# A mixture-of-experts layer on one core: biases by row groups, the remainder's matmuls in three batches, and TensorE in program order

## The chip, the core and the metric

The kernel runs on one core of a Trainium2 chip (trn2) and uses its TensorE (matmuls, PE in the profile; its weight loads are PEld), VectorE (DVE), ScalarE (ACT), GpSimd (POOL) and SyncE (SP, which starts the weight loads). The metric is the device time in microseconds of one execution, the median of several runs.

## What is computed

One layer over 1024 latent tokens of width 1024: a mixer (gated linear attention and pooling), and then a mixture of experts, and a final RMSNorm. The change is in the mixture of experts, 32 experts of which each token takes four:

```python
def expert_block(args):
    xblk, e = args
    gu = xblk @ w_gu[e] + b_gu[e]                 # 1024 x 2048
    gate, up = jnp.split(gu, 2, axis=-1)
    gate = jnp.minimum(gate, SWIGLU_LIMIT)
    up = jnp.clip(up, -SWIGLU_LIMIT, SWIGLU_LIMIT)
    act = (up + 1.0) * gate * jax.nn.sigmoid(SWIGLU_ALPHA * gate)
    return act @ w_down[e] + b_down[e]            # 1024 x 1024
```

The results are weighted by the softmax of the token's four router logits and added up token by token.

## The kernel before, in words

The mixer takes about the first 530 us. What follows is the loop of experts, written out 33 times in Python: turn `e` does gate/up of expert `e` and down of expert `e-1`.

**Experts by rank.** The experts are sorted by their number of tokens, on the chip. The 16 largest are called heavy here, the others light; the loop takes them in the order `HHHLLH`, then `LH` twelve times, then `LL`. Each has a main block of 128 tokens. A heavy one has a remainder of 32 tokens more as well, the first expert two of them.

**The main block.** Weights come in chunks of 1 MB, eight for gate/up and four for down, into a ring of eight buffers (`load_to`). Each chunk is split into a high and a low part of type fp32r: a copy on ACT (L131), a subtraction on DVE (L132), into one of three buffers `hl` (`split_to`). A chunk then takes 12 matmuls of 128x128 by 128x512, three for each product (`mm3`), into `pG` (four PSUM banks) or `pD` (two).

**The remainder.** Its 32 tokens use the array's columns in four groups of 32: four matmuls stand side by side, each with a quarter of the output's columns, into `pR` (one bank). It multiplies the unsplit chunks (`RAW`), every two chunks in gate/up and with every chunk in down. An fp32 matmul appears as two records.

**The biases.** `ball` holds the three bf16 parts of `b_gu` for all experts on 96 partitions. At the start of each expert four matmuls of 128 rows (`onehot` by `ball`) put the bias into `pG` (`gu_start`, L1480), and four in column groups into `pR`.

**Transposes and routing.** Inputs come by an indirect gather on POOL (`xg`, `xq`); `prep_x` transposes them for the next expert, `prep_a` the last expert's activation. Every block of transposes, and every routing result (`prep_route`, tile `pq`), lands in the single bank of the pool `ptr`: a block of four transposes is copied by ACT (L1393) and then subtracted by DVE (L1394), and only after this may TensorE write the bank again.

**What sets the order.** A scheduler places each engine's instructions by readiness on a simulated clock, and among ready ones by their place in the program. `T.strict` makes each TensorE instruction follow the one traced before it on that engine. It is on in parts of the mixer and in the last turn (`e == NE`), and off in the rest of the loop. Turn `e`, in the program's text: the bias; then for each of eight chunks `k` the matmuls, followed at k = 0, 1, 2 by `prep_a` of expert e-1, at k = 3, 4, 5 by `prep_x` of expert e+1, at k = 6 by the selection and at k = 7 by the routing of expert e+2; then the four down blocks of expert e-1, ahead of whose first stands the activation of expert e (`act`), and `finish_e` with a scatter on POOL. Ahead of the loop stand the gathers, `route_weights` (`px`, `pyw`, and three casts on ACT) and the weights' routing for the first two experts.

Of the kernel before, what the change touches and what calls it, by code (L numbers as in the profile page):

```python
# [9 lines left out]
F32 = mybir.dt.float32  # L10
# [42 lines left out]
def tile_hybrid_layer(ctx: ExitStack, tc: tile.TileContext, x, c, ctx_in, c_ctx, w_ada, b_ada, norm_mix_w,  # L53
# [867 lines left out]
        V.memset(jcol[32 * j:32 * j + 32], float(j))  # L921
    emod = rp.tile([P, 1], F32, name="emod")
    V.scalar_tensor_tensor(emod, jcol, -32.0, pcol, op0=ALU.mult, op1=ALU.add)
    jeq = rp.tile([P, 4], F32, name="jeq")
    V.tensor_scalar(jeq, io[:, 0:4], jcol, None, op0=ALU.is_equal)
    ltm = rp.tile([P, NE], F32, name="ltm")
# [377 lines left out]
    h2d4 = h2d.rearrange("t (j n) -> (t j) n", j=4)  # L1304
    nslot = [0]

    slots = RS + [MS[0], MS[2], MS[3]] + RX

    def wslot():
# [63 lines left out]
    def slot_weights(i, pq):  # L1373
        n = 1 + nrem[i]
        wc = xp.tile([P, 3], F32, name="wc", tag="wc", bufs=4)
        V.tensor_reduce(wc[:, :n], pq[:, :n, 2:5], axis=mybir.AxisListType.X, op=ALU.add)  # L1376
        R["wc", i] = wc
# [54 lines left out]
        if e > 0:  # L1432
            stream += [("dn", e - 1, k) for k in range(0, KT, 2)]
    RAW, HL, EV = {}, {}, {}
    AHEAD_LOAD, AHEAD_SPLIT = 7, 2
    pos_load, pos_split = [0], [0]

    def load_to(n):
# [29 lines left out]
    def onehot(i, n):  # L1468
        return ohp[:, order[i]:order[i] + 1].to_broadcast([P, n])

    def gu_start(e):
        g = pgu.tile([P, 4, 512], F32, name="pG", tag="g")
        rs = []
        if nrem[e]:
            rs.append(prm.tile([P, 512], F32, name="pR", tag="r"))
        if nrem[e] > 1:
            rs.append(pdn.tile([P, 2, 512], F32, name="pR1", tag="d")[:, 0])
        GU[e] = (g, rs)
        for n in range(4):
            T.matmul(g[:, n], onehot(e, P), ball[:, n * 512:n * 512 + 512], start=True, stop=False)  # L1480
        bf = ball[:, 0:2048].rearrange("p (h n) -> p h n", h=2)
        for r in rs:
            for j in range(4):
                T.matmul(r[32 * j:32 * j + 32], onehot(e, CAPR), bf[:, :, 256 * j:256 * j + 256],
                         start=True, stop=False)

    def gu_chunk(e, k):
        g, rs = GU[e]
        xT = R["xT", e]
        hl = HL.pop(("gu", e, k))  # L1490
        for n in range(4):
            mm3(g[:, n], xT[:, 0, k], xT[:, 1, k], hl[:, 0, n * 512:n * 512 + 512],
                hl[:, 1, n * 512:n * 512 + 512], False, k == KT - 1)
        if k % 2 == 0:
            return
        raws = [RAW.pop(("gu", e, q)).rearrange("p (h n) -> p h n", h=2) for q in (k - 1, k)]
        for r, xq in zip(rs, R["xqT", e]):
            for i, raw in enumerate(raws):
                for j in range(4):
                    T.matmul(r[32 * j:32 * j + 32], xq[:, i, 32 * (k // 2):32 * (k // 2) + 32],  # L1500
                             raw[:, :, 256 * j:256 * j + 256], start=False, stop=(k == KT - 1 and i == 1))

    def act_unit(gate, up, w, tag, bufs):
        g = ap.tile([P, w], F32, name="ag", tag="ag" + tag)
        t = ap.tile([P, w], F32, name="at", tag="at" + tag, bufs=bufs)
        V.tensor_scalar(g, gate, 7.0, None, op0=ALU.min)
        S.activation(g, g, AF.Gelu_apprx_sigmoid)
        V.tensor_scalar(t, up, 1.0, -6.0, op0=ALU.add, op1=ALU.max)
        V.scalar_tensor_tensor(t, t, 8.0, g, op0=ALU.min, op1=ALU.mult)
        return t  # L1510

    def act(e):
        g, rs = GU.pop(e)
        R["act", e] = act_unit(g[:, 0:2].rearrange("p a n -> p (a n)"), g[:, 2:4].rearrange("p a n -> p (a n)"),
                               D, "m", 1)
        R["actq", e] = [act_unit(r[:, 0:256], r[:, 256:512], 256, "r", 2) for r in rs]

    def dn_start(e):
        d = (pgu.tile([P, 4, 512], F32, name="pDl", tag="g")[:, 2:4] if e == NE - 1 else
# [7 lines left out]
    def dn_chunk(e, k0):  # L1527
        d, rs = DN[e]
        aT = R["aT", e]
        raw = RAW.pop(("dn", e, k0)).rearrange("p (k n) -> p k n", n=D)  # L1530
        hl = HL.pop(("dn", e, k0)).rearrange("p h (k n) -> p h k n", n=D)
        for u in range(2):
            k = k0 + u
            for n in range(2):
                mm3(d[:, n], aT[:, 0, k], aT[:, 1, k], hl[:, 0, u, n * 512:n * 512 + 512],
                    hl[:, 1, u, n * 512:n * 512 + 512], k == 0, k == KT - 1)
        for g, (r, aq) in enumerate(zip(rs, R["aqT", e])):
            for u in range(2):
                for j in range(4):
                    T.matmul(r[32 * j:32 * j + 32], aq[:, u, 32 * (k0 // 2):32 * (k0 // 2) + 32],  # L1540
                             raw[:, u, 256 * j:256 * j + 256], start=(g == 0 and k0 + u == 0), stop=(k0 + u == KT - 1),
                             skip_group_check=True)

    def finish_e(e):
        d, rs = DN.pop(e)
# [31 lines left out]
    def final_tables():  # L1577

        F["y"] = ap.tile([P, 2, D], F32R, name="yhl", tag="aT")
        F["to"] = xp.tile([P, D], F32R, name="to", tag="xg2", bufs=1)  # L1580
        row = ap.tile([P, D], F32, name="trow", tag="agm")
        G.iota(row.bitcast(I32), pattern=[[1, D]], base=0, channel_multiplier=0)
        ixf = xp.tile([P, 1], F32, name="ixf")
        V.tensor_copy(ixf, R["ix", NE - 1])
        V.tensor_copy(row, row.bitcast(I32))
        V.tensor_scalar(F["to"], row, ixf, None, op0=ALU.is_equal)

        F["fw"] = ap.tile([P, D], F32, name="fw", tag="asm")
        nc.sync.dma_start(F["fw"], final_norm_w[None, :].broadcast_to([P, D]))
        st = F["st"] = xp.tile([P, 2, D], F32R, name="wb", tag="xT")  # L1590
        S.activation(st[0:96, 1], bdg, AF.Copy)
        G.tensor_tensor(st[32:64, 1], bdg[32:64], st[32:64, 1].bitcast(F32), op=ALU.subtract)
        w3 = ap.tile([P, NT, 3, NE], F32, name="w3", tag="y")
        S.activation(w3, lgn[:, :, None, :].to_broadcast([P, NT, 3, NE]), AF.Copy)
        F["w3"] = w3
# [70 lines left out]
    with tc.high_priority():  # L1666
        for i in range(2):
            if i == 0:
                prep_sel(0, (slice(0, P), slice(P, P + CAPR * nrem[0])))
            pq = ptr.tile([P, 3, 8], F32, name="pq", tag="t")  # L1670
            route_main(i, pq, slice(0, 2))
            gather_main(i, pq)
            if i == 0:
                prep_sel(1, (slice(0, CAP0 + CAPR * nrem[1]),))
            pq = pdn.tile([P, 3, 8], F32, name="pqr", tag="d")
            route_rem(i, pq, slice(5, 7))
            gather_rem(i, pq)
            if i == 0:
                load_to(1)

                tc.keep_in_program_order(G.memset(slots[(nslot[0] + 1) % 8][0:1, 0:1], 0.0))
                load_to(2)
        pinned[0] = True
        split_to(1)
        pinned[0] = False
        for p_ in range(3):
            prep_x(0, p_)
    route_weights()
    dump("posm", posm)
    dump("wfull", lg)  # L1690
    for i in range(2):
        pq = ptr.tile([P, 3, 8], F32, name="pq", tag="t")
        route_main(i, pq, slice(2, 5))
        route_rem(i, pq, slice(2, 5))
        slot_weights(i, pq)
    for e in range(nexp + 1):
        if e < nexp:
            gu_start(e)
            for k in range(KT):
                advance()  # L1700
                gu_chunk(e, k)
                if e > 0 and k < 3:
                    prep_a(e - 1, k)
                if e + 1 < NE and 3 <= k < 6:
                    prep_x(e + 1, k - 3)
                if e + 2 < NE and k == 6:
                    prep_sel(e + 2)
                if e + 2 < NE and k == 7:
                    prep_route(e + 2)
        T.strict = e == NE  # L1710
        if e > 0:
            dn_start(e - 1)
            for k0 in range(0, KT, 2):
                advance()
                with tc.high_priority() if e == NE - 1 else ExitStack():
                    if k0 == 0 and e < nexp:
                        act(e)
                    if e == NE - 1 and k0 >= 2:
                        prep_a(e, k0 // 2 - 1)
                dn_chunk(e - 1, k0)  # L1720
                if e == NE:
                    (final_tables, lambda: final_weights(0), lambda: final_weights(1), int)[k0 // 2]()
            finish_e(e - 1)
            if e == NE - 1:
                final_rows()
        elif nexp:
            act(e)
            route_blocks()
# [152 lines left out]
```

## Time and profile before

| | us |
|---|---|
| median of three runs (2027.07 to 2027.38) | 2027.13 |
| the profiled execution | 2027.01 |
| its span, first to last instruction | 2025.2 |
| PE busy | 1927.8 |
| DVE busy | 1553.9 |
| ACT busy | 1142.8 |
| POOL busy | 339.5 |

Mean granted TensorE clock over the span: 0.974 of full speed. A row of a timeline has the start (us from the span's start), the length of a run of like instructions, engine, line, operation, output tile and inputs, shape and count; in square brackets the engine's idle time ahead of it and what ended it. Ends of matmuls are modelled and overlap, so starts are compared. Some matmul records are missing (one of the four bias matmuls of an expert, for one).

### The profile page before, as it was taken

What the parts mean: (1) busy time and instruction counts of PE and PEld (TensorE: products, weight loads), DVE (VectorE), ACT (ScalarE), POOL (GpSimd) and SP (SyncE); (2) the same over time, 40 slices, a digit from 0 to 9 for tenths busy, and PEclk for the clock granted to TensorE, in tenths of its full rate; (3) what the DMA queues carried; (4) which work ended last, traced back from release to release, by engine and by line L of the source; (5) the groups of instructions that cost most, each with busy time, mean ns of one, the idle gap of its engine ahead of it and who ended that gap; (6) DMA issues with size and microseconds to landing.
All of it is one profiled execution on the core that took longest, in us unless ns stands there. A gap on an engine that the chain in (4) does not pass through costs nothing.

```text
span 2025.2 us, 29313 instructions
## 1 busy us (share of the span) xinstructions
PE 1927.8 (95%) x11361; PEld 1383.1 (68%) x11393; DVE 1553.9 (77%) x1599; ACT 1142.8 (56%) x1264; POOL 339.5 (17%) x241
## 2 busy tenths in 40 slices
PE   7999998998699999999999999999999999999985
PEld 4776775776465677767676676767667676776764
DVE  4486478568776788879788887978878797887886
ACT  4464556644453466656565565656556565655663
POOL 2010043013301111101111110111211111111113
PEclk9999999998699999999999999999999999999997
DMA  9274422243556798978879797887979788797874
GB/s 350 70 294 183 151 75 90 77 166 106 221 218 259 269 337 317 361 272 318 333 263 363 270 363 278 318 331 258 367 274 356 282 319 331 254 372 272 349 262 178
DMA packets 125480, 532.85 MB, mean 263 GB/s; under 512 B 13180, under 2 KB 27312, under 8 KB 90424
## 3 DMA queue, kind: packets, MB, share of 16 engines
q1 hardware_dynamic: 109416, 482.35, 61.9%
q0 software_dynamic: 15344, 48.01, 9.0%
q8 instruction: 91, 1.49, 0.3%
q10 hardware_dynamic: 576, 0.56, 0.1%
q14 instruction: 53, 0.43, 0.1%
HBM read 498.21 MB, written 32.67 MB: 262 GB/s over the span
## 4 chain that ended last, share of the span: by engine, by line
PE 87%; DVE 6%; ACT 2%; issue 2%; DMA 2%; POOL 1%; SPq 0%; POOLq 0%; DVEq 0%; ACTq 0%
PE pG L74 37%; PE pD L74 17%; PE pa L74 13%; PE pR L74 11%; PE pps L79 3%; PE pw L74 2%; PE pt L74 2%; DVE hl L132 1%; PE pt L79 1%; ACT hl L131 1%; PE pDl L74 1%; PE pq L74 1%; DMA ring<-in_w_ada_dram 0%; DMA mix<-in_w_ada_dram 0%; DVE ra L719 0%
## 5 line engine op out<-in xcount | busy, mean ns | idle before, releaser
L74 PE MATMUL pG<-hl,xT 128*128 128x512 f32 x3072 | 765.1, 401 | 0.7 <-ACT xT L1393 0.7
L74 PEld LDWEIGHTS pG<-hl,xT 128*128 128x128 f32 x3072 | 565.8, 188 | 166.5 <-issue 28.9
L132 DVE TENSOR_TENSOR hl<-ring,hl 128x2048 fp32r<-128x2048 f32 (+2 forms) x199 | 397.1, 2008 | 157.9 <-ACT hl L131 156.4
L131 ACT ACTIVATE hl<-ring 128x2048 fp32r<-128x2048 f32 (+2 forms) x199 | 331.5, 1668 | 265.6 <-PE pG L74 136.2
L131 ACT ACTIVATE hl<-mix 128x2048 fp32r<-128x2048 f32 (+1 forms) x146 | 277.5, 1902 | 208.0 <-PE pG L74 103.4
L132 DVE TENSOR_TENSOR hl<-mix,hl 128x2048 fp32r<-128x2048 f32 x144 | 329.7, 2291 | 73.0 <-ACT hl L131 71.5
L74 PE MATMUL pD<-hl,aT 128*128 128x512 f32 x1488 | 380.3, 404 | 0.9 <-ACT aT L1393 0.7
L74 PEld LDWEIGHTS pD<-hl,aT 128*128 128x128 f32 x1488 | 277.8, 189 | 85.5 <-ACT xT L1393 10.9
L132 DVE TENSOR_TENSOR hl<-ringx,hl 128x2048 fp32r<-128x2048 f32 x96 | 221.7, 2309 | 43.9 <-ACT hl L131 43.9
L131 ACT ACTIVATE hl<-ringx 128x2048 fp32r<-128x2048 f32 x96 | 184.5, 1922 | 99.8 <-PE pG L74 56.3
L1559 POOL DMA_INDIRECT acc<-y,ix x31 | 78.2, 2521 | 903.1 <-DVE y L1554 873.5
L74 PE MATMUL pa<-hl,hi 128*128 128x512 f32 x544 | 181.0, 420 | 6.0 <-DVE wsg L760 3.7
L74 PEld LDWEIGHTS pa<-hl,hi 128*128 128x128 f32 x544 | 103.1, 198 | 32.0 <-DVE wsg L760 4.8
L74 PE MATMUL pa<-hl,lo 128*128 128x512 f32 x272 | 109.3, 415 | 6.0 <-DVE lo L818 6.0
L74 PE MATMUL pa<-hi,hl 128*128 128x512 f32 (+1 forms) x288 | 95.8, 396 | 1.0 <-ACT hi L400 1.0
L1355 POOL DMA_INDIRECT xg<-h2d,ix x32 | 67.8, 2120 | 143.3 <-DVE wc L1376 130.5
L1393 ACT ACTIVATE aT<-pps 128x512 fp32r<-128x512 f32 x62 | 36.4, 587 | 63.7 <-PE pps L79 63.7
L1564 POOL DMA_INDIRECT acc<-yq,ixr x17 | 43.8, 2579 | 152.3 <-DVE hl L132 75.1
L74 PEld LDWEIGHTS pa<-hi,hl 128*128 128x128 f32 x288 | 55.1, 193 | 16.3 <-issue 2.7
L74 PEld LDWEIGHTS pa<-hl,lo 128*128 128x128 f32 x272 | 53.3, 199 | 18.8 <-DVE lo L818 6.4
L74 PE MATMUL pR<-ring,xqT 128*32 128x512 f32 x408 | 65.8, 599 | 0.0
L1394 DVE TENSOR_TENSOR aT<-pps,aT 128x512 fp32r<-128x512 f32 x62 | 42.5, 685 | 19.7 <-ACT aT L1393 19.7
(386 smaller groups left out, 2119.2 us busy)
## 6 DMA issues: line engine op xcount, KB each, us to landing
ring<-in_w_gu_dram SPq DMA_DIRECT2D x96, 1024.0 KB
mix<-in_w_gu_dram SPq DMA_DIRECT2D x96, 1024.0 KB
ringx<-in_w_gu_dram SPq DMA_DIRECT2D x64, 1024.0 KB
ring<-in_w_down_dram SPq DMA_DIRECT2D x48, 1024.0 KB
mix<-in_w_down_dram SPq DMA_DIRECT2D x48, 1024.0 KB
ringx<-in_w_down_dram SPq DMA_DIRECT2D x32, 1024.0 KB
ring<-in_w_in_dram SPq DMA_DIRECT2D x32, 512.0 KB
ring<-in_w_ada_dram SPq DMA_DIRECT2D x16, 1024.0 KB
```

The costliest lines, as they stand in the source:

```text
L74: i = nc.tensor.matmul(*a, **k)
L79: i = nc.tensor.transpose(*a, **k)
L131: S.activation(hl[:, 0], src, AF.Copy)
L132: i = eng.tensor_tensor(hl[:, 1], src, hl[:, 0].bitcast(F32), op=ALU.subtract)
L1355: nc.gpsimd.indirect_dma_start(out=xg, out_offset=None, in_=h2d, in_offset=bass.IndirectOffsetOnAxis(ap=ix[:, 0:1], axis=0))
L1393: S.activation(dst[:, 0, part], pp, AF.Copy)
L1394: V.tensor_tensor(dst[:, 1, part], pp, dst[:, 0, part].bitcast(F32), op=ALU.subtract)
L1559: nc.gpsimd.indirect_dma_start(out=acc, out_offset=bass.IndirectOffsetOnAxis(ap=ix[:, 0:1], axis=0), in_=y, in_offset=None, compute_op=ALU ...
L1564: nc.gpsimd.indirect_dma_start(out=acc4, out_offset=bass.IndirectOffsetOnAxis(ap=ixr[g][:, 0:1], axis=0), in_=yq, in_offset=None, compute_ ...
```

## The change

- `bias_rows` is new. Once, ahead of the loop, it sorts the biases by rank with matmuls: `bq[32 n + 4 j + i, q]` is part i of columns 512 n to 512 n + 511 of the bias of rank 8 q + j. `gu_bias` then adds an expert's bias by four matmuls of 32 rows each, in four row groups and four banks, behind chunk 1 (light) or 3 (heavy).
- The remainder's gate/up matmuls run in two batches, behind chunks 3 and 7, the first together with their bias; those of down in one batch behind the last block.
- So the ring's buffers are free later, and loads run five chunks ahead in place of seven in the program's text.
- The remainder's activation comes ahead of the main one.
- `T.strict` is on from the loop's start to its end.
- Routing of expert e+2 stands behind the second down block of turn e (from e = 1 on).
- `fw` shares the buffer of `bq`.

```diff
+    rsel = rp.tile([P, 2, 8], F32, name="rsel")
+    rhot = rp.tile([P, 8], BF16, name="rhot")
...
+    V.scalar_tensor_tensor(rhot, rsel[:, 0], 4.0, rsel[:, 1], op0=ALU.is_lt, op1=ALU.mult)
...
+    bq = ap.tile([P, 4, 512], BF16, name="bq", tag="bq")
+    def bias_rows():
+        perm = tp.tile([P, NE, 4], BF16, name="perm")
+        V.memset(perm, 0.0)
+        for i in range(3):
+            V.tensor_copy(perm[32 * i:32 * i + 32, :, i], eqr[32 * i:32 * i + 32])
+        flat = perm.rearrange("p r i -> p (r i)")
+        for q in range(4):
+            pb = ptr.tile([P, 512], F32, name="pbq", tag="t")
+            for n in range(4):
+                T.matmul(pb[32 * n:32 * n + 32], flat[0:96, 32 * q:32 * q + 32], ball[0:96, n * 512:n * 512 + 512],
+                         start=True, stop=True)
+            S.activation(bq[:, q], pb, AF.Copy)
...
-    AHEAD_LOAD, AHEAD_SPLIT = 7, 2
+    AHEAD_LOAD, AHEAD_SPLIT = 5, 2
...
-        for n in range(4):
-            T.matmul(g[:, n], onehot(e, P), ball[:, n * 512:n * 512 + 512], start=True, stop=False)
...
+    def gu_bias(e):
+        g, rs = GU[e]
+        q, j = divmod(order[e], 8)
         for n in range(4):
+            rows = slice(32 * n, 32 * n + 32)
+            T.matmul(g[:, n], rhot[rows, j:j + 1].to_broadcast([32, P]), bq[rows, q], start=False, stop=False)
...
-                hl[:, 1, n * 512:n * 512 + 512], False, k == KT - 1)
-        if k % 2 == 0:
+                hl[:, 1, n * 512:n * 512 + 512], k == 0, k == KT - 1)
+        if k == (3 if rs else 1):
+            gu_bias(e)
+        if k % 4 < 3:
             return
...
+            if k == 3:
                 for j in range(4):
+                    T.matmul(r[32 * j:32 * j + 32], onehot(e, CAPR), bf[:, :, 256 * j:256 * j + 256],
+                             start=True, stop=False)
+            for q, raw in raws:
...
     def act(e):
         g, rs = GU.pop(e)
+        R["actq", e] = [act_unit(r[:, 0:256], r[:, 256:512], 256, "r", 2) for r in rs]
         R["act", e] = act_unit(g[:, 0:2].rearrange("p a n -> p (a n)"), g[:, 2:4].rearrange("p a n -> p (a n)"),
                                D, "m", 1)
-        R["actq", e] = [act_unit(r[:, 0:256], r[:, 256:512], 256, "r", 2) for r in rs]
...
+        if k0 < 6:
+            return
+        raws = [RAW.pop(("dn", e, q)).rearrange("p (k n) -> p k n", n=D) for q in (0, 2, 4, 6)]
...
-        F["fw"] = ap.tile([P, D], F32, name="fw", tag="asm")
+        F["fw"] = ap.tile([P, D], F32, name="fw", tag="bq")
...
+    bias_rows()
     route_weights()
...
+    T.strict = True
     for e in range(nexp + 1):
...
-                if e + 2 < NE and k == 7:
+                if e + 2 < NE and k == 7 and e == 0:
                     prep_route(e + 2)
-        T.strict = e == NE
...
                 dn_chunk(e - 1, k0)
+                if k0 == 2 and e + 2 < NE:
+                    prep_route(e + 2)
```

## Rows read from the trace of the kernel before

**Rows 1.** The page's part 1: each engine's busy time, share, instructions.

```profile
PE 1927.8 (95%) x11361; PEld 1383.1 (68%) x11393; DVE 1553.9 (77%) x1599; ACT 1142.8 (56%) x1264; POOL 339.5 (17%) x241
```

**Rows 2.** By stretch, one period: engines' busy us, clock, DMA share, GB/s.

```profile
884.66:973.11 88.45, 88.35 (x512) 62.64 (x513) 72.75 (x52) 53.11 (x38) 12.40 (x7) 1.00 0.84 312
```

**Rows 3.** Timeline of PE, this period: three chunks ahead of transposes.

```profile
932.19 8.63 PE L74 MATMUL pG<-hl,xT 128*128 128x512 f32 x36
940.66 0.60 PE L79 MATMUL pps<-ident,at 128*128 128x128 f32 x4
```

**Rows 4.** The same timeline: the remainder's bias between two blocks of transposes.

```profile
960.96 0.60 PE L79 MATMUL pps<-ident,xg 128*128 128x128 f32 x4
961.32 4.44 PE L74 MATMUL pG<-hl,xT 128*128 128x512 f32 x18
965.69 0.40 PE L74 MATMUL pR<-mix,ohp 128*32 128x512 bf16 x4
966.02 2.84 PE L74 MATMUL pG<-hl,xT 128*128 128x512 f32 x11
968.69 0.38 PE L79 MATMUL ppr<-ident,xq 128*128 128x128 f32 x2
```

**Rows 5.** The same timeline: a bias, a down block, the next transposes.

```profile
913.07 1.04 PE L74 MATMUL pG<-mix,ohp 128*128 128x512 bf16 x3
913.75 3.15 PE L74 MATMUL pD<-hl,aT 128*128 128x512 f32 x12
916.74 0.60 PE L79 MATMUL pps<-ident,xg 128*128 128x128 f32 x4
```

**Rows 6.** The same timeline: first and last gate/up remainder, last down remainder.

```profile
884.95 1.92 PE L74 MATMUL pR<-ring,xqT 128*32 128x512 f32 x16
...
906.13 1.06 PE L74 MATMUL pR<-ring,xqT 128*32 128x512 f32 x6
...
959.40 1.07 PE L74 MATMUL pR<-ring,aqT 128*32 128x256 f32 x16
```

**Rows 7.** Timeline of all engines: transposes, their bank held long.

```profile
1020.25 1.92 ACT L131 ACTIVATE hl<-mix 128x2048 fp32r<-128x2048 f32 x1 [0.88 <-PE pG L74]
1020.28 0.60 PE L79 MATMUL pps<-ident,at 128*128 128x128 f32 x4
...
1022.07 0.58 ACT L1393 ACTIVATE aT<-pps 128x512 fp32r<-128x512 f32 x1
1022.19 2.29 DVE L132 TENSOR_TENSOR hl<-mix,hl 128x2048 fp32r<-128x2048 f32 x1 [0.43 <-ACT hl L131]
...
1024.40 0.69 DVE L1394 TENSOR_TENSOR aT<-pps,aT 128x512 fp32r<-128x512 f32 x1
```

**Rows 8.** Timeline of all engines: other transposes, bank held briefly.

```profile
889.79 0.60 PE L79 MATMUL pps<-ident,at 128*128 128x128 f32 x4
...
891.06 0.69 DVE L1394 TENSOR_TENSOR aT<-pps,aT 128x512 fp32r<-128x512 f32 x1 [1.45 <-ACT aT L1393]
```

**Rows 9.** Timeline of PE where the loop of experts begins.

```profile
543.02 1.22 PE L74 MATMUL pG<-hl,xT 128*128 128x512 f32 x2 [0.74 <-ACT xT L1393]
...
548.66 0.44 PE L79 MATMUL ppr<-ident,xq 128*128 128x128 f32 x2 [0.24 <-ACT xqT L1400]
...
558.76 0.61 PE L74 MATMUL pyw<-pbd,wT 128*128 128x128 f32 x4
...
570.51 0.92 PE L74 MATMUL pq<-info,sel 128*128 128x3 bf16 x72
...
576.99 0.65 PE L74 MATMUL pq<-info,sel 128*128 128x3 bf16 x40
```

**Rows 10.** DMA issues: tiles, queue and count, us from issue to landing.

```profile
xg<-h2d,ix POOLq DMA_INDIRECT x32, 10.6
```

**Rows 11.** Waits of SP in the loop: us in total, times, longest.

```profile
SPq L1446 <- PE pR L74: 505.9, 124, 22.5
```

**Rows 12.** Tile pG, a reader: ns min/median/max, first and last start.

```profile
L1506 DVE TENSOR_SCALAR ag<-pG x32: 1202/1217/1224, 585.7 to 1958.2; 128x1024 f32<-128x1024 f32 x32
```

More of the change, by code (lines that the diff above doesn't have):

```diff
@@ L923, in tile_hybrid_layer @@
     V.scalar_tensor_tensor(emod, jcol, -32.0, pcol, op0=ALU.mult, op1=ALU.add)
+    rsel = rp.tile([P, 2, 8], F32, name="rsel")
+    rhot = rp.tile([P, 8], BF16, name="rhot")
+    V.scalar_tensor_tensor(rsel[:, 0], io[:, 0:8], -4.0, emod.to_broadcast([P, 8]), op0=ALU.mult, op1=ALU.add)
+    V.tensor_scalar(rsel[:, 1], rsel[:, 0], 0.0, None, op0=ALU.is_ge)
+    V.scalar_tensor_tensor(rhot, rsel[:, 0], 4.0, rsel[:, 1], op0=ALU.is_lt, op1=ALU.mult)
     jeq = rp.tile([P, 4], F32, name="jeq")
@@ L1478, in gu_start @@
         GU[e] = (g, rs)
+    def gu_bias(e):
+        g, rs = GU[e]
+        q, j = divmod(order[e], 8)
         for n in range(4):
-            T.matmul(g[:, n], onehot(e, P), ball[:, n * 512:n * 512 + 512], start=True, stop=False)
[L1481 to L1485, printed above, removed]
+            rows = slice(32 * n, 32 * n + 32)
+            T.matmul(g[:, n], rhot[rows, j:j + 1].to_broadcast([32, P]), bq[rows, q], start=False, stop=False)
     def gu_chunk(e, k):
@@ L1492, in gu_chunk @@
             mm3(g[:, n], xT[:, 0, k], xT[:, 1, k], hl[:, 0, n * 512:n * 512 + 512],
-                hl[:, 1, n * 512:n * 512 + 512], False, k == KT - 1)
-        if k % 2 == 0:
+                hl[:, 1, n * 512:n * 512 + 512], k == 0, k == KT - 1)
+        if k == (3 if rs else 1):
+            gu_bias(e)
+        if k % 4 < 3:
             return
-        raws = [RAW.pop(("gu", e, q)).rearrange("p (h n) -> p h n", h=2) for q in (k - 1, k)]
+        raws = [(q, RAW.pop(("gu", e, q)).rearrange("p (h n) -> p h n", h=2)) for q in range(k - 3, k + 1)]
+        bf = ball[:, 0:2048].rearrange("p (h n) -> p h n", h=2)
         for r, xq in zip(rs, R["xqT", e]):
-            for i, raw in enumerate(raws):
+            if k == 3:
                 for j in range(4):
-                    T.matmul(r[32 * j:32 * j + 32], xq[:, i, 32 * (k // 2):32 * (k // 2) + 32],
-                             raw[:, :, 256 * j:256 * j + 256], start=False, stop=(k == KT - 1 and i == 1))
+                    T.matmul(r[32 * j:32 * j + 32], onehot(e, CAPR), bf[:, :, 256 * j:256 * j + 256],
+                             start=True, stop=False)
+            for q, raw in raws:
+                for j in range(4):
+                    T.matmul(r[32 * j:32 * j + 32], xq[:, q % 2, 32 * (q // 2):32 * (q // 2) + 32],
+                             raw[:, :, 256 * j:256 * j + 256], start=False, stop=(q == KT - 1))
     def act_unit(gate, up, w, tag, bufs):
@@ L1529, in dn_chunk @@
         aT = R["aT", e]
-        raw = RAW.pop(("dn", e, k0)).rearrange("p (k n) -> p k n", n=D)
         hl = HL.pop(("dn", e, k0)).rearrange("p h (k n) -> p h k n", n=D)
@@ L1536, in dn_chunk @@
                     hl[:, 1, u, n * 512:n * 512 + 512], k == 0, k == KT - 1)
+        if k0 < 6:
+            return
+        raws = [RAW.pop(("dn", e, q)).rearrange("p (k n) -> p k n", n=D) for q in (0, 2, 4, 6)]
         for g, (r, aq) in enumerate(zip(rs, R["aqT", e])):
-            for u in range(2):
+            for k in range(KT):
                 for j in range(4):
-                    T.matmul(r[32 * j:32 * j + 32], aq[:, u, 32 * (k0 // 2):32 * (k0 // 2) + 32],
-                             raw[:, u, 256 * j:256 * j + 256], start=(g == 0 and k0 + u == 0), stop=(k0 + u == KT - 1),
-                             skip_group_check=True)
+                    T.matmul(r[32 * j:32 * j + 32], aq[:, k % 2, 32 * (k // 2):32 * (k // 2) + 32],
+                             raws[k // 2][:, k % 2, 256 * j:256 * j + 256],
+                             start=(g == 0 and k == 0), stop=(k == KT - 1), skip_group_check=True)
     def finish_e(e):
```

## The prediction, made before the changed kernel was run

> **What bounds the kernel now.** I read the page's busy times by engine first, then those of one stretch of the loop of experts, then TensorE's timeline in one period of that loop, and last, in the timeline of all engines, how long a transposed block holds the one PSUM bank it lands in.
>
> TensorE is busy for nearly all of the span [rows 1]. Inside the loop it has no gap: 88.35 of 88.45 us [rows 2]. That is one period, a heavy expert and a light one; there are 16 such pairs. DVE is busy for 72.75 us of the same stretch and the DMA share is 0.84. So the loop is worth what TensorE's own work is worth, as long as nothing makes TensorE stand. The scheduler brought this about: it lets TensorE take whatever is ready, and so puts a transposed block where its bank has long been free. Ahead of the transposes at 940.66 stand three chunks, 36 matmuls [rows 3], since the transposes before them, though the program text has one chunk there. From these rows one matmul takes (940.66 - 932.19)/36 = 0.235 us and a chunk of 12 takes 2.82; a block of four transposes takes 961.32 - 960.96 = 0.36 us [rows 4].
>
> **What the change takes away.** A pair now holds:
> - two biases of four full-width matmuls. From 913.07 to 916.74 are 3.67 us; less 12 x 0.235 that is 0.85 us for one [rows 5], 0.21 a matmul;
> - visits to 32-column mode. From 960.96 to 968.69 are 7.73 us; less 0.36 and 29 x 0.235 the four small bf16 matmuls cost 0.555 us [rows 4]. They run side by side, so they stream for 0.21 and the way in and out costs 0.345. I count nine such visits in the period: five with gate/up remainders, from 884.95 to 906.13 and broken up by transposes, one with routing, two with down remainders, the later at 959.40 [rows 6], and the one with the remainder's bias at 965.69 [rows 4].
>
> After it a heavy expert has two gate/up batches (the first holds the bias) and one down batch, and routing keeps its visit: four in place of nine. 5 x 0.345 = 1.73 us. The remainder matmuls themselves stay as many.
>
> The trace has no bias of four row groups with bf16. I bound it below by 0.21 (all four at once, no way in or out) and above by 4 x 0.21 + 0.345 = 1.19 (no overlap at all). I take 0.555, the same four matmuls side by side in columns [rows 4], which is the nearest row. That saves 0.295 for each expert, 0.59 a pair. Together 2.32 us a pair, **-37 us** over 16.
>
> A page states that price too. The Trainium skill, "TensorE: Matmul & The Clock Gate", Part 3, tells of four row tiles (32 rows, 512 columns) that ran 3.07 times as fast as one after another. By it the bias would cost an estimated 0.85/3.07 = 0.28 us, and the total would lie 9 us lower. No run here shows it.
>
> **What the fixed order adds, in the loop.** All transposes and routing share the one bank of pool ptr. In program order one chunk lies between the blocks for k = 0 and 1 (the activation's two halves) and between those for k = 3 and 4 (the next expert's input). So the second wants the bank 0.36 + 2.82 = 3.18 us after the first began. The trace shows when it is free: the block begins at 1020.28, ACT has begun the next split 0.03 us before (the chunk's end freed its buffer), copies at 1022.07, DVE takes that split's subtraction first and ends the block's at 1024.40 + 0.69 [rows 7]. That is 4.81 us, and TensorE in a fixed order would stand for 1.63. The bound from below is nothing: at 889.79 DVE was through after 1.96 us [rows 8], because no split had begun. I take 4.81, since in the fixed order every block comes right behind a chunk, as there, and each chunk's end starts a split. Places:
> - k = 0 to 1, experts 1 to 31: 15 heavy ones at 1.63; 16 light ones with the bias between, 1.63 - 0.555 = 1.08. Together 42 us.
> - k = 3 to 4: in heavy experts the batch lies between chunk and block, so the split is over: nothing. 15 light ones at 1.63: 25 us.
> - the remainder's transposes behind these (k = 2 and 5), 32 places between nothing and 1.63: while TensorE stood, ACT and DVE worked off the split, so I take a quarter of a us, 8 us.
>
> Together **+75 us**, between 0 and 119.
>
> **And ahead of the loop.** The first pinned matmul stands behind the last one traced before it, the second expert's routing for the weights. Now the first expert's gate/up begins at 543.02 while that routing comes at 570.51 and 576.99 [rows 9]. Its chain must now end first: bias_rows' four rounds through the same bank (a block of four small matmuls 0.4 [rows 4], a copy of 128x512 0.6 [rows 7], two hops: some 1.2 each, half of them in the wait for the first gather), px and pyw, then 11.75 us from pyw to the first routing (three casts, two subtractions, two splits between them on ACT), then 2 us of routing. From the last small transposes at 548.66 that makes 549 + 2.4 + 1.5 + 11.75 + 2 = 567, or 24 us late. Some 3 us of that work stood inside the first expert, and its loads and splits will be ready, which I put at 4. I take **+17**, between 10 (casts alone) and 31 (the chain no faster than it was, 577.6).
>
> **Edits I cost at nothing.** Routing for expert e+2 goes two down blocks later: its matmuls, then DVE's index (behind an operation of the activation and a split's, up to 3 us) and POOL's gather, ahead of this expert's scatter as before. Its first use is two down blocks and four chunks on, 6 x 2.82 = 17 us; a gather took 10.6 us from issue to landing (the median) [rows 10], so 3 us are left; without them each late us costs 31. The remainder's activation first: three short DVE operations ahead of the main one, hidden by the 11 us of down work ahead of the next gate/up. Loads five ahead in place of seven: buffers free in fours behind a batch. SP already waits for remainder matmuls, 124 times for gate/up alone [rows 11], and a batch of four chunks (11.3 us) covers four loads of 1 MB at the 312 GB/s of [rows 2] but for 2 us; four more chunks lie ready then. The final weight's row only loads later, some 50 us ahead of its use. The three small DVE operations for rhot are in the 17.
>
> **Sum.** 2025.2 us of span, 1.8 around it: 2027.0, as the median of the runs, 2027.1. -37 + 75 + 17 = +55: **2082 us**.
>
> **The rivals.**
> A, faster. The stalls hang on one order: DVE takes the split's subtraction ahead of the block's. Where DVE is more than 0.6 us behind when the split comes, the block's, which is earlier in the program, is ready too and goes first; the bank is then free in about 3 us and nothing stands. Against it: in the period DVE idles for 16 us. For it: a faster TensorE leaves it less, and the releases differ by 2.9 us already [rows 7, 8]. It decides below some 0.7 us of stall per place. With none of the 75 us the time is 2027 - 37 + 17 = 2007, or 2000 with the short way into the loop, and 1990 if that way costs nothing.
> B, no change: stalls of about 20 us in all, 2027.
> C, slower still. DVE falls behind in down: three operations of the activation and one like them for y, 1.22 us each [rows 12], and four splits of 2.29 [rows 7] are 14.0 us against 11.3 of matmuls. Two splits made ahead cover the 2.7 us; where that lead is gone, up to 1 us for each expert comes on top, about 2110. Or the row groups do not run side by side, so the change does not do what it says: 32 x (1.19 - 0.555) = 20 us more, 2102.
>
> **How the numbers follow.** The forecast has 0.53, A 0.30, B 0.05, C 0.12. Slower by over 0.2% (4 us, about what a measurement of this kernel can tell) takes the forecast and C. The range reaches down through most of A to 1992 and up to 2106, short of C's worst; the forecast's own range is 2050 to 2105.
>
> **What would show it.** Right: TensorE's waits name pps behind the DVE subtraction L1394, 1 to 1.7 us each, some 45 times; a pair takes about 90 us in place of 88.45, with 86 of work; the first gate/up begins near 565; four 32-column visits a pair. Wrong: TensorE still busy for all of a period, of 86 us; or the waits name hl, xg or the loads.

## The result and the profile after

The kernel after takes **2081.45 us** (median of 4 runs, 2080.88 to 2083.54) against 2027.1 before: 1.0269 times as long, 95% interval 1.0256 to 1.0282. The forecast was 2082. The sum came out within 1 us, but its terms did not: the saved work was larger than its term, the added time was larger too, and part of it had no term; the errors cancelled. The times of the experiments below are medians too, that of e11 without one run of 4667.8 us.

Busy time by engine, the page's first part of the kernel after; it answers to [rows 1]:

```profile
span 2079.1 us, 29348 instructions
...
PE 1878.8 (90%) x11409; PEld 1372.6 (66%) x11409; DVE 1552.2 (75%) x1606; ACT 1146.5 (55%) x1268; POOL 361.9 (17%) x241
```

TensorE works 49 us less than before and takes 54 more. So it stands for some 100 us more. What for, the waits of TensorE in the kernel after (what it waited for: us in total, times, longest):

```profile
PE pps L79 <- DVE aT L1416: 51.0, 31, 2.3
PE pps L79 <- DVE xT L1416: 27.0, 16, 1.7
...
PE pps L79 <- DVE at L1539: 6.6, 1, 6.6
PE pw L79 <- ACT w L1626: 6.2, 1, 6.2
...
PE pq L74 <- ACT info L1248: 5.4, 1, 5.4
PE ppr L79 <- DVE xT L1416: 4.8, 3, 1.7
...
PE pblk L74 <- DVE nbb L1269: 4.2, 1, 4.2
```

The first two rows are the wait that was forecast: a block of transposes waits for the one bank until DVE has subtracted the block before. One of the 16 in the second row (1.5 us) stands ahead of the loop; in the loop it is 76.5 us in 46 places. The single waits below are at the loop's entry and end.

Busy time by stretch, before (from the fourth expert's gate/up to the last, and from there to the end) and after (one pair; then the same two stretches); the columns are us, then busy us of PE, PEld, DVE, ACT and POOL, the granted clock, the DMA share and GB/s:

```profile
705.61:1956.80 1251.19, 1249.61 (x7139) 892.99 (x7164) 1033.24 (x720) 757.90 (x526) 196.28 (x85) 1.00 0.84 315
1956.80:2025.20 68.40, 39.06 (x161) 30.22 (x159) 48.78 (x35) 28.71 (x33) 22.50 (x21) 0.79 0.46 170
```

```profile
898.75:988.72 89.97, 84.94 (x517) 61.67 (x513) 72.63 (x52) 53.14 (x37) 15.52 (x6) 1.00 0.81 307
...
723.17:2002.88 1279.71, 1205.45 (x7171) 879.92 (x7168) 1029.34 (x718) 757.80 (x525) 219.08 (x84) 1.00 0.82 309
2002.88:2079.09 76.21, 42.41 (x160) 32.96 (x159) 48.25 (x35) 28.83 (x33) 22.09 (x21) 0.78 0.45 166
```

This is the whole account of 54 us. Up to the fourth expert it is 723.17 - 705.61 = **+17.6**. In the loop TensorE's work falls by 44.2 and its standing rises from 1.6 to 74.3, together **+28.5**. The end is **+7.8** longer. A pair takes 89.97 in place of 88.45 [rows 2], 5.0 of it standing.

One light expert in the loop, the timeline of the kernel after (start, us, engine, operation; in brackets the idle time before it and what ended it):

```profile
947.58 0.60 PE L79 MATMUL pps<-ident,at 128*128 128x128 f32 x4
947.78 1.92 ACT L131 ACTIVATE hl<-ring 128x2048 fp32r<-128x2048 f32 x1 [0.88 <-PE pG L74]
947.79 2.28 DVE L132 TENSOR_TENSOR hl<-ringx,hl 128x2048 fp32r<-128x2048 f32 x1
...
949.60 0.58 ACT L1415 ACTIVATE aT<-pps 128x512 fp32r<-128x512 f32 x1
949.99 2.28 DVE L132 TENSOR_TENSOR hl<-ring,hl 128x2048 fp32r<-128x2048 f32 x1
...
950.91 0.39 PE L74 MATMUL pG<-bq,rhot 32*128 32x512 bf16 x4
...
952.19 0.68 DVE L1416 TENSOR_TENSOR aT<-pps,aT 128x512 fp32r<-128x512 f32 x1
...
952.93 0.66 PE L79 MATMUL pps<-ident,at 128*128 128x128 f32 x4 [1.62 <-DVE aT L1416]
```

The block begins at 947.58. ACT's copy of it is done at 949.60 + 0.58 = 950.18, but DVE took up a split at 949.99 and comes to the block at 952.19. The bank is free at 952.87, 5.29 us after the block began, in place of the 4.81 of [rows 7], and the bias in between (four matmuls side by side, 0.39 us) does not hide the rest.

### The profile page after: what moved, and what is told of

The parts are those of the page before. It is cut to its first block, busy times and chain, and to the rows that moved or that the text cites. A ratio compares the mean times of both kernels' runs of the same rounds, so it can differ in the third digit from the quotient of the medians.

```text
span 2079.1 us, 29348 instructions
## 1 busy us (share of the span) xinstructions
PE 1878.8 (90%) x11409; PEld 1372.6 (66%) x11409; DVE 1552.2 (75%) x1606; ACT 1146.5 (55%) x1268; POOL 361.9 (17%) x241
## 4 chain that ended last, share of the span: by engine, by line
PE 67%; DVE 15%; issue 9%; ACT 7%; DMA 1%; POOL 1%; DVEq 0%; SPq 0%; POOLq 0%; ACTq 0%
PE pG L74 26%; PE pa L74 12%; PE pD L74 11%; PE pR L74 9%; DVE hl L132 6%; ACT hl L131 6%; PE pps L79 2%; PE pw L74 2%; PE pt L74 2%; DVE aT L1416 1%; DVE sel L1348 1%; PE pt L79 1%; DVE xT L1416 1%; DMA mix<-in_w_ada_dram 0%; PE ppr L79 0%
## 5 line engine op out<-in xcount | busy, mean ns | idle before, releaser
L132 DVE TENSOR_TENSOR hl<-ring,hl 128x2048 fp32r<-128x2048 f32 (+2 forms) x199 | 397.9, 2007 | 168.3 <-ACT hl L131 167.1
L74 PE MATMUL pD<-hl,aT 128*128 128x512 f32 x1488 | 365.5, 400 | 0.2 <-DVE hl L132 0.2
L1377 POOL DMA_INDIRECT xg<-h2d,ix x32 | 62.1, 1940 | 895.7 <-DVE ix L1373 439.3
L1591 POOL DMA_INDIRECT acc<-y,ix x31 | 104.5, 3370 | 176.7 <-DVE y L1586 176.7
L79 PE MATMUL pps<-ident,at 128*128 128x128 f32 x256 | 40.6, 282 | 57.6 <-DVE aT L1416 51.0
L79 PEld LDWEIGHTS pps<-ident,at 128*128 128x128 f32 x256 | 29.6, 141 | 73.6 <-DVE aT L1416 62.3
L1415 ACT ACTIVATE xT<-pps 128x512 fp32r<-128x512 f32 x64 | 37.7, 588 | 59.1 <-PE pps L79 56.5
L79 PE MATMUL pps<-ident,xg 128*128 128x128 f32 x256 | 41.1, 284 | 30.7 <-DVE xT L1416 27.0
L79 PEld LDWEIGHTS pps<-ident,xg 128*128 128x128 f32 x256 | 29.9, 143 | 55.3 <-DVE xT L1416 33.9
```

What stands on the lines that cost most here:

```text
L74: i = nc.tensor.matmul(*a, **k)
L79: i = nc.tensor.transpose(*a, **k)
L132: i = eng.tensor_tensor(hl[:, 1], src, hl[:, 0].bitcast(F32), op=ALU.subtract)
L1377: nc.gpsimd.indirect_dma_start(out=xg, out_offset=None, in_=h2d, in_offset=bass.IndirectOffsetOnAxis(ap=ix[:, 0:1], axis=0))
L1415: S.activation(dst[:, 0, part], pp, AF.Copy)
L1591: nc.gpsimd.indirect_dma_start(out=acc, out_offset=bass.IndirectOffsetOnAxis(ap=ix[:, 0:1], axis=0), in_=y, in_offset=None, compute_op=ALU ...
```

## The experiments

Ten kernels were built on one of the two and timed in turn with the kernel before (2027.2 to 2027.8 us in each group).

**e1, the order undone.**

```diff
-    T.strict = True
     for e in range(nexp + 1):
...
+        T.strict = e == NE
```

> The kernel after, with TensorE's order in the loop left to the scheduler again (the last turn as before); row-group biases, the batches in the program text, five loads ahead and the later routing stay. By its instruction list the scheduler cuts the batches up again: 132 groups of remainder matmuls in the loop where the kernel before has 138 and the kernel after 48. My theory (the order costs some 105 us in stalls and at its two ends, and it is also what keeps the batches whole): no waits on pps, first gate/up near 545, of the 37 us of saved work only the bias is left, 32 x 0.3 to 0.46 = 9 to 15 us: 2010 to 2020. Rival 1 (batches pay without the order too): 1985 to 1995. Rival 2 (the cost is in the other edits, shorter load-ahead, later routing or bias rows): 2060 to 2085.

Measured: 2027.24 us, 1.0001 (0.9991 to 1.0010) of before. Neither theory's number. The stalls are gone, so the order makes them, but so is most of what the work saved: a pair takes 88.0, against 88.45 [rows 2].

```profile
875.90:963.90 88.00, 87.89 (x515) 62.33 (x512) 72.97 (x52) 52.87 (x37) 15.46 (x7) 1.00 0.85 313
```

The batches of the program text are only batches if TensorE runs them in the text's order: in the trace, other matmuls part the remainder's into 107 groups in e1 and 120 in the kernel before, but 49 in the kernel after. So the two halves of this change can't be priced apart from each other in a free order.

**e2, the order alone**, on the kernel before.

```diff
+    T.strict = True
     for e in range(nexp + 1):
...
-        T.strict = e == NE
```

> The kernel before with nothing but TensorE in program order from the loop's start; remainder after every second chunk, full-width biases at an expert's start, routing behind the last chunk. My theory (order alone makes the stalls: a block follows a block after one chunk): waits on pps behind DVE of 1 to 1.7 us in 40 to 50 places, a pair of 92 to 94 us, first gate/up 15 to 22 us late: 2100 to 2150. Rival (the stalls come with the changed work, that is with batches that free loads and splits in bursts): waits on pps under 20 us in all, only the entry is dear: 2045 to 2060.

Measured: 2108.32 us, 1.0393 (1.0376 to 1.0411), the theory's time. The stalls need none of the changed work.

```profile
PE pps L79 <- DVE aT L1394: 27.3, 16, 1.7
PE pps L79 <- DVE xT L1394: 27.0, 16, 1.7
PE pD L74 <- DVE hl L132: 10.8, 14, 1.2
```

```profile
905.54:997.40 91.86, 87.55 (x511) 61.27 (x513) 72.67 (x52) 53.27 (x37) 13.28 (x7) 1.00 0.82 300
```

In the loop there are 31 such waits, not 46: here a heavy expert has a batch between its first two blocks. A second reading is new: TensorE works 87.55 us in this pair against 88.35 [rows 2] on the same matmuls. The order as such saves it 0.8 us of work.

**e4, two chunks between blocks.**

```diff
-                if e > 0 and k < 3:
-                    prep_a(e - 1, k)
-                if e + 1 < NE and 3 <= k < 6:
-                    prep_x(e + 1, k - 3)
+                if e > 0 and k in (0, 2):
+                    prep_a(e - 1, k // 2)
+                if e + 1 < NE and k in (4, 6):
+                    prep_x(e + 1, k // 2 - 2)
+                if e < 2 and k == 7:
+                    prep_x(1, 2) if e == 0 else prep_a(0, 2)
...
                 dn_chunk(e - 1, k0)
+                if k0 == 0 and e + 1 < NE:
+                    prep_x(e + 1, 2)
+                if k0 == 4 and 1 < e < NE:
+                    prep_a(e - 1, 2)
```

> The kernel after with the same blocks of transposes two chunks apart in the program text: the activation's halves behind gate/up chunks 0 and 2, the next input's behind 4 and 6, the remainders' transposes in down. Nothing else. My theory (the one bank of the transposes comes free 4.8 to 5.1 us after a block begins; with two chunks the next block wants it after 6.0): the 78 us of waits on pps are gone, a pair takes 85 us, first gate/up as late as in the kernel after: 1998 to 2010. Rival 1 (ACT or DVE can't keep up and the wait moves to the splits hl): a pair of 88 to 90, 2050 to 2080. Rival 2 (half comes back as waits on xg or the loads): 2025 to 2045.

Measured: **1992.64 us**, 0.9824 (0.9807 to 0.9840) of before, 89 us below the kernel after. No wait for the bank is left in the loop, and none came in its place:

```profile
880.57:965.05 84.48, 84.48 (x516) 61.90 (x512) 72.55 (x52) 52.66 (x37) 14.20 (x6) 1.00 0.86 327
...
716.90:1918.00 1201.10, 1198.89 (x7171) 883.00 (x7168) 1028.14 (x718) 751.05 (x525) 203.42 (x84) 1.00 0.87 329
```

TensorE stands for 2.2 us in 1201. My theory holds, with a time 5 us below its range; both rivals fall, though DVE is busy for 86% of the pair. The pair's 84.48 is also the clean price of the work: 3.97 us less than before's 88.45 [rows 2].

**e5, only DVE's order.** A block's subtraction goes ahead of the split's behind it; by the traces, the orders of TensorE, ACT and POOL are those of the kernel after.

```diff
-        V.tensor_tensor(dst[:, 1, part], pp, dst[:, 0, part].bitcast(F32), op=ALU.subtract)
+        i = V.tensor_tensor(dst[:, 1, part], pp, dst[:, 0, part].bitcast(F32), op=ALU.subtract)
+        if pinned[0]:
+            tc.keep_in_program_order(i)
...
     for e in range(nexp + 1):
+        pinned[0] = 0 < e < NE - 1
...
-        split_to(ci + AHEAD_SPLIT)
+        split_to(ci + AHEAD_SPLIT + pinned[0])
```

> The kernel after with one thing moved, DVE's order: a block's subtraction stands ahead of the split's that follows that chunk's end, where the kernel after has it behind. TensorE's and ACT's orders are the same as after. My theory (the block's subtraction is held up by the split's 2.28 us ahead of it in DVE's order, and that makes the stall): the bank is free 3.0 to 3.2 us after a block begins, waits on pps under 15 us in place of 78, 2005 to 2020. Rival 1 (the split, now 0.7 us later, is what TensorE waits for next): waits on hl of 20 to 70 us, 2030 to 2075. Rival 2 (ACT's copy behind ACT's cast is the holder): waits on pps stay above 50 us, 2060 to 2085.

Measured: 2029.02 us, 1.0003 (0.9993 to 1.0013) of before, 52 us below the kernel after. The timeline of the same place, a light expert, and TensorE's longest wait:

```profile
934.29 0.60 PE L79 MATMUL pps<-ident,at 128*128 128x128 f32 x4
...
936.31 0.58 ACT L1415 ACTIVATE aT<-pps 128x512 fp32r<-128x512 f32 x1
936.92 0.69 DVE L1416 TENSOR_TENSOR aT<-pps,aT 128x512 fp32r<-128x512 f32 x1
937.53 2.28 DVE L132 TENSOR_TENSOR hl<-ring,hl 128x2048 fp32r<-128x2048 f32 x1
937.61 0.39 PE L74 MATMUL pG<-bq,rhot 32*128 32x512 bf16 x4
...
937.94 0.66 PE L79 MATMUL pps<-ident,at 128*128 128x128 f32 x4
```

```profile
PE pD L74 <- DVE hl L132: 20.3, 15, 1.6
```

DVE is at the block 0.03 us after ACT's copy, the bank is free 3.3 us after the block began, and the next block starts without a wait. So DVE's order is what makes the stall, as the theory says. But the theory's time is missed by 9 us: the split that was passed over is late in down, 20.3 us in 15 places, which is rival 1 at its lower bound. A pair takes 86.8, 2.3 more than in e4; 1.6 of it is this wait.

**e6 and e7, the fixed order for turns 1 to 30 only**, on e4 and on the kernel after.

```diff
-    T.strict = True
     for e in range(nexp + 1):
+        T.strict = 0 < e < NE - 1
...
+        T.strict = 0 < e < NE - 1 or e == NE
         if e > 0:
             dn_start(e - 1)
```

> The kernel with the blocks two chunks apart (e4), and TensorE's fixed order kept for turns 1 to 30 only: the first expert's gate/up with the route_blocks traced behind it, and turn 31, are left to the scheduler as in the kernel before (the very last turn is fixed in both). My theory (the entry costs 22 to 24 us, route_blocks 5 and more at half clock, the last expert's activation and final weights 8 to 13): first gate/up near 545, last gate/up to end of the span 68 us, 1953 to 1966. Rival (the late entry hides work that must be done anyway, and the loop is then waiting for splits or gathers): first gate/up near 545, but 1975 to 1990.

> The kernel after with TensorE's fixed order kept for turns 1 to 30 only, its blocks one chunk apart as they are. My theory (stalls in the loop and costs of the ends are separate and add): the waits on pps behind DVE stay at 70 to 78 us, 35 to 39 us less at the ends: 2042 to 2050. Rival (the two overlap; the stalls absorb part of the ends' cost): 2055 to 2075.

Measured: e6 **1981.03 us**, 0.9772 (0.9759 to 0.9785) of before, 12 below e4; e7 2064.95, 1.0185 (1.0169 to 1.0201), 16 below the kernel after. Both times are the rivals'; the reason put to e7's, that the stalls in the loop absorb it, is not what happened, since e6 has none. In e6, from the first gate/up to the fourth expert, and the end:

```profile
543.40:710.20 166.80, 153.47 (x1108) 98.39 (x1108) 114.39 (x121) 83.53 (x67) 16.23 (x9) 0.94 0.64 241
...
1910.90:1979.20 68.30, 39.04 (x162) 30.14 (x160) 49.14 (x35) 28.71 (x33) 22.47 (x21) 0.81 0.53 198
```

The end's 7 us come back in full: 68.30, as before. Of the entry little does. The first gate/up begins at 543.40 (543.02 before), but TensorE then stands 13 us inside the stretch, and the fourth expert begins at 710.20, 6.7 earlier than in e4 and 4.6 later than before. The waits moved from ahead of the first expert to behind it:

```profile
594.61 0.92 PE L74 MATMUL pq<-info,sel 128*128 128x3 bf16 x72 [4.26 <-ACT info L1248]
...
599.85 1.12 PE L79 MATMUL pps<-ident,xg 128*128 128x128 f32 x4 [1.41 <-DVE xT L1416]
...
608.38 0.31 PE L74 MATMUL pblk<-linc,nbb 32*32 32x32 f32 x2 [3.27 <-DVE nbb L1269]
```

**e8, full-width biases** and **e9, a batch behind each chunk**, both on e4.

```diff
-            T.matmul(g[:, n], rhot[rows, j:j + 1].to_broadcast([32, P]), bq[rows, q], start=False, stop=False)
+            T.matmul(g[:, n], onehot(e, P), ball[:, n * 512:n * 512 + 512], start=False, stop=False)
```

```diff
-        if k % 4 < 3:
-            return
-        raws = [(q, RAW.pop(("gu", e, q)).rearrange("p (h n) -> p h n", h=2)) for q in range(k - 3, k + 1)]
+        raws = [(q, RAW.pop(("gu", e, q)).rearrange("p (h n) -> p h n", h=2)) for q in (k,)]
...
-            if k == 3:
+            if k == 0:
```

> The kernel with the blocks two chunks apart (e4), and the bias as four full-width matmuls at the same place; bias_rows is still run ahead of the loop. My prediction's term (0.85 against 0.555, 32 times): 9 us more than e4, 2001 to 2003. The rows of the kernel after (the four row groups end 0.75 us behind the chunk's last matmul, of which the way in and out is most): as much or less, 3 to 9 us. By the Trainium skill's factor of three: 18 us, 2010 to 2012.

> The kernel with the blocks two chunks apart (e4), and the gate/up remainder behind each chunk in place of each four: the same matmuls, eight visits to 32-column mode in a heavy expert in place of two. Down stays in one batch. My prediction's term (0.345 us a visit, 96 more): 33 us, 2023 to 2028. Rival 1 (a visit costs nothing, TensorE overlaps it): under 5 us. Rival 2 (each visit also drains what stands behind, 0.5 us and more): 2040 to 2055.

Measured: e8 2005.46 us (ratio 0.9892, 0.9876 to 0.9907), 12.8 over e4, which makes 0.40 us for each of 32 biases. e9 2035.57 us (1.0040, 1.0024 to 1.0055), 42.9 over e4, 0.45 for each of 96 visits. One pair of e8, and one of e9:

```profile
883.00:968.40 85.40, 85.40 (x516) 62.41 (x512) 72.59 (x52) 52.66 (x37) 14.21 (x6) 1.00 0.86 323
```

```profile
891.40:978.50 87.10, 86.65 (x516) 60.97 (x512) 72.37 (x52) 52.76 (x37) 14.21 (x6) 1.00 0.84 318
```

By the pairs it is (85.40 - 84.48)/2 = 0.46 a bias and (87.10 - 84.48)/6 = 0.44 a visit. Both are over the terms of the prediction, 0.295 and 0.345. e8's time lies between that of the prediction's term and that of the factor of three, e9's between its forecast and rival 2. The factor of three of the Trainium skill ("TensorE: Matmul & The Clock Gate", Part 3) would have made the bias's gain an estimated 18 us. It agrees as far as the four row groups do run side by side (0.39 us from the first's start to the last's end, above), but the gain is 13. That the way into their mode and out of it makes the difference is not shown by itself.

**e10 and e11, the entry again.** e10 is e6 with bias_rows moved behind the first two experts' slot weights; e11 is e10 with the fixed order from turn 2.

```diff
-    bias_rows()
     route_weights()
...
         slot_weights(i, pq)
+    bias_rows()
```

```diff
-        T.strict = 0 < e < NE - 1
+        T.strict = 1 < e < NE - 1
```

> The kernel e6 (blocks two chunks apart, fixed order for turns 1 to 30) with bias_rows moved behind route_weights and the first two experts' slot weights in the program. In e6 the rounds of bias_rows took the transposes' one bank ahead of px and pyw, which came at 579 and 585 in place of 554 and 559, and TensorE stood for them at the end of the first expert; the second began at 608.8 against 588.9 before. My theory (that order is the whole delay): px near 555, the routing of the weights near 570, second expert at 592 to 600, 1965 to 1974. Rival (the first expert's free order leaves the next input's blocks for the end whatever stands first): second expert at 604 or later, 1975 to 1985.

> As e10, and TensorE's fixed order begins one turn later, with the third expert, so that the second expert's blocks, its routing and route_blocks can go between matmuls as in the kernel before. My theory (what is left of the entry's cost is the fixed order of turn 1): second expert at 589 to 593, third within 61 us of it as before, 1958 to 1968. Rival (in a free turn 1 the batches are cut up and visits cost what the waits did): within 4 us of e10.

Measured: 1983.00 us (0.9782, 0.9769 to 0.9794) and 1984.08 (0.9789, 0.9776 to 0.9801): no better than e6, and both times the rivals'. In e10 the routing of the weights comes at 572.63, near the 570 expected, and the second expert still begins at 608.0; TensorE now waits ahead of it for DVE's part of a block:

```profile
572.63 0.92 PE L74 MATMUL pq<-info,sel 128*128 128x3 bf16 x72
...
599.01 1.12 PE L79 MATMUL pps<-ident,xg 128*128 128x128 f32 x4 [5.63 <-DVE xT L1416]
```

In e11 the second expert begins at 594.4, but the third at 662.7, where it begins in e6 (662.6) and e10 (662.8) too; before it was 650.8. So my theory fell twice: what I moved was late, but was not what set the third expert. From the second expert's first gate/up to the third's, e11 and then e6:

```profile
594.39:662.75 68.36, 60.67 (x425) 38.91 (x425) 47.58 (x67) 28.55 (x24) 8.42 (x4) 0.93 0.42 147
```

```profile
608.83:662.57 53.74, 53.27 (x377) 36.29 (x375) 39.38 (x44) 27.45 (x21) 5.45 (x2) 0.97 0.48 180
```

e11 is 14.4 us ahead when the second expert begins, and loses it there again: 7.4 us to more work (the remainder's matmuls stand in seven groups, in e6 in three), as its rival has it, and 7.2 to standing, most of it in one wait for DVE's part of a block:

```profile
651.79 0.59 PE L79 MATMUL ppr<-ident,at 128*128 128x128 f32 x2 [5.15 <-DVE xT L1416]
```

What would bring the third expert to 650.8 again was not found; these 12 us stay open.

## Why the prediction was right, and by which steps

**What bounds the kernel: right.** e4 shows it from the other side: with the waits away its span is 85.7 us shorter than that of the kernel after, 79.0 of them TensorE's standing. The five loads ahead and the later routing, costed at nothing, are in e4 too, where no wait for loads or gathers is left from the fourth expert on.

**The saved work: too small.** The prediction put it at 2.32 us a pair; e4 shows 3.97. Five visits at 0.44 (e9) are 2.2, two biases at 0.46 (e8) 0.9. The third part, some 0.8, was no step of the prediction: in the free order a chunk's eight remainder matmuls are cut in the middle too, and then no longer all run side by side. In the timeline of before, the eight records on `ring` are two at 904.60, and the other six at 906.13 [rows 6], behind a block; the two take 1.02 us and the six 1.06, each as long as the whole eight on `ringx`:

```profile
903.71 1.06 PE L74 MATMUL pR<-ringx,xqT 128*32 128x512 f32 x8
904.60 1.02 PE L74 MATMUL pR<-ring,xqT 128*32 128x512 f32 x2
```

e2, where none is cut, works 0.8 less per pair than before with one visit more, which would make this part 1.2: the size agrees only roughly. In the kernel after itself the pair works 84.94, and from the fourth expert on 44 us of its work came off.

**The stalls: right in kind, near in sum, not in each place.** Heavy experts stand 1.70 where 1.63 was forecast, the light ones' second input block 1.70 (1.63). The light ones' second activation block stands 1.62, not 1.08: the prediction let the bias hide 0.555 of a fixed 4.81, but DVE runs two splits in a row there and the bank is free after 5.29. The remainder's transposes were put at 8 us; in the loop they wait three times, 5.5. That makes 82 where 75 stood.

**The entry: +17.6 where 17 stood, by luck.** The first gate/up begins at 564.93 (forecast 567). Not seen was `route_blocks`, whose matmuls are traced behind the first expert and now stand in line ahead of the second:

```profile
609.46 0.19 PE L74 MATMUL pcs<-crow,eqr 32*32 32x1 f32 x2 [0.97 <-DVE wc L1398]
613.85 0.31 PE L74 MATMUL pblk<-linc,nbb 32*32 32x32 f32 x2 [4.20 <-DVE nbb L1269]
...
614.30 4.76 PE L74 MATMUL pG<-hl,xT 128*128 128x512 f32 x12
```

So the delay grows from 21.9 to 25.4 us at the second expert, and shrinks again to 17.6 by the fourth. From the first gate/up to the fourth expert, before and after:

```profile
543.02:705.61 162.59, 158.34 (x1089) 97.13 (x1093) 111.42 (x119) 80.45 (x63) 14.33 (x8) 0.97 0.69 264
```

```profile
564.93:723.17 158.24, 144.22 (x986) 94.44 (x974) 105.48 (x113) 73.02 (x54) 13.95 (x8) 0.96 0.55 205
```

TensorE stands 9.8 us more there and works 14.1 less. Some 3 of these 14 went ahead of the loop, as forecast; the rest is saved work of three heavy experts, which the prediction has in its -37. The 4 us that it took off for loads and splits being ready were hardly there to gain: before, TensorE stood for 0.3 us in the whole first expert.

**The end: missed.** It was costed at nothing, without a word on turn 31, where the blocks of the last activation and the transposes of the final weights now also wait in line (6.6 and 6.2 us in the list above). Before, too, TensorE stood there; now it stands 33.8 us in place of 29.3. Behind the two waits a chunk each ran slowly (below), and the work takes 42.4 us in place of 39.1. That is the 7.8.

**The rivals.** A had the right lever, DVE's order, and the wrong condition and price. That order is fixed before the kernel runs and shows the same in each pair: at 947.79 DVE was behind with a split, and still took the next one ahead of the block. e5 had to change it in the program. With it changed the time is 2029, not 2007, because the split then comes late. Nor does the 0.7 us per place at which A was to decide follow from the prediction's terms: the 20 us of B over 46 places are 0.43. Of C, the row groups do run side by side, and DVE is late in down in e2 (10.8 us) and e5 (20.3), but not in the kernel after. B had nothing for it.

**The sum: luck.** From the first gate/up to the last, TensorE's work falls by 14.1 + 44.2 = 58.3 us, where the prediction had 37, and 3 for work that goes ahead of the loop. Against these 18 us stand three errors the other way: TensorE stands for 9.8 + 72.7 = 82.5 us more (`route_blocks` included) where 75 was forecast, the first gate/up comes 21.9 us later where 24 - 4 was, and the end has 7.8 more. They come to 17, so 2082 and 2081.45 agree within 1 us.

## What to carry to other kernels

An order fixed for one gain (batches kept whole) fixes everything else that shares the engine: list what stands behind what, bank by bank, before pinning it. If one buffer serves a chain of blocks, compare the time from a block's start to its release (here 4.8 to 5.3 us, most of it in the queues of ACT and DVE) with the work that stands between two of them; moving the blocks to twice that distance was worth 89 us and cost nothing. And an edit that only pays in a given order should be timed in that order: alone, neither half of this change made the kernel faster.

## What was not expected of the hardware

After waits of 4 to 7 us TensorE ran slower for a while. The granted clock in the kernel after (the third number from a row's end), right behind the waits of 4.20 and 6.63 us:

```profile
614.30:618.90 4.60, 4.60 (x14) 3.61 (x13) 2.54 (x18) 0.00 (x0) 0.00 (x0) 0.59 0.96 388
...
2012.30:2019.00 6.70, 6.70 (x23) 5.52 (x24) 4.03 (x3) 2.32 (x3) 3.45 (x2) 0.61 0.02 4
```

That is mostly the lower level of 1.2 GHz: the rows of these chunks of 12 matmuls last 4.76 and 5.09 us, where one at full clock lasts 3.04. So some 1.7 us more came behind the wait of 4.20 us. Behind the 1.6 to 1.7 us stalls in the loop nothing of the kind shows: the clock of the pair is 1.00.
